# Two more pairs of early products at the head of each SwiGLU, and left factors of the first down group kept whole

## The chip, the cores and the metric

The kernel runs on one core of a Trainium2 chip. The metric is the device time of one execution in microseconds (us). TensorE is called PE below, its weight loads PEld; VectorE is DVE, ScalarE is ACT, GpSimd is POOL, and SP is the engine whose queue issues the DMAs.

## The reference, cut to what matters

One encoder block on x of 1024 tokens by 1024 columns, all in float32: a SwiGLU with an RMS norm before and after it, a mixer of two attentions, and a second SwiGLU of the same form.

```python
def swiglu(x, w_gate, w_up, w_down):          # 1024 -> 2816 -> 1024
    return (jax.nn.silu(x @ w_gate) * (x @ w_up)) @ w_down

f1 = swiglu(rms_norm(h, ffn1_pre_g), ffn1_w_gate, ffn1_w_up, ffn1_w_down)
h = h + 0.5 * rms_norm(f1, ffn1_post_g)
mix = hybrid_mixer(rms_norm(h, mix_pre_g), ...)
h = h + rms_norm(mix, mix_post_g)
f2 = swiglu(rms_norm(h, ffn2_pre_g), ffn2_w_gate, ffn2_w_up, ffn2_w_down)
h = h + 0.5 * rms_norm(f2, ffn2_post_g)
```

## The kernel before

**Splits and seven products.** Every float32 factor is split into a rounded high part and a rest (ACT copies the high part, DVE or POOL subtracts it), and a product takes three matmuls: high by high, high by rest, rest by high. Both SwiGLUs (`ffn`, called once for each) use a scheme of seven products of half blocks in place of eight (the Strassen kind): products 0 to 6 of sums and differences of the quarters.

**Gate and up.** The 2816 hidden columns are 11 pieces `p` of 256. A unit `(p, m)` is the gate (m = 0) or up (m = 1) weight of one piece; `units` lists the 22 of them. Each unit has seven products of 12 matmuls of 512 columns (L675). Products 0 and 1 need only blocks 0 and 1 of the transposed input, made from tokens 0 to 511; the other five need blocks 2 to 6, made from tokens 512 to 1023 and from differences (L414, transposes L426, rests L431). `seq` is the order of the products on PE: at its start products 0 and 1 of the first two units, then unit by unit. `loads` brings the weights of a unit in two halves of 512 KB (`raw_tok` bounds how many), `combos` makes the sums of weight quarters on DVE (L615, L619, L622, L626), `one` makes a split weight `wt` (ACT L648, DVE L649; `w_tok` bounds how many). `step` adds the partial results: a copy of product 0 (`m1`, L744), then L760, L771, L780, L793 and L800 on DVE. `unit_tok` lets two units be open.

**Hidden values.** `hidden` takes the finished quarters of a piece, makes their sums (L849 to L851, L856), splits the seven left factors of the down product (ACT L825, DVE L828) and stores them as high part and rest in the DRAM tensor `hs` (L829, 512 KB each).

**Down.** Five groups `g` of two pieces, seven products each, in the order 0, 5, 1, 4, 6, 2, 3; each has four token tiles `tt` of six matmuls (L1079). `left` loads a factor `ha` (1 MB, L942), `right` splits a weight `wdb` (ACT L521, POOL L522) out of `rawd` (L900) or of sums `td` (DVE L919 to L929). The large buffers that `ha` and `wdb` take are those that the input blocks held, so a first-group factor can be loaded when the last unit has used a block. `evac` adds the products into `acc` and `bacc` (L1026, L1028). After the last product of the last group `fix` adds `bacc` to three quarters: one on DVE (L1037), two at once on POOL (L1039). The eleventh piece is a plain product (L1103 on, its additions L1118), then comes the norm behind the SwiGLU (`postnorm`: L488, L499, L307, L309, L512).

**What sets the order.** The program is written by a planner (`Plan`): processes ask for an engine with a rank (low first) and an assumed duration, and the order in which they are served becomes the instruction order of each engine. Each engine then runs its list in order: an instruction that waits holds up all behind it. In `ffn`, weight splits and combinations have rank 7, the input's chain rank 3, `left` rank 6, `right` rank 7.

Of the kernel before, what the change touches and what calls it, by code (L numbers as in the profile page):

```python
# [19 lines left out]
P = 128  # L20
# [90 lines left out]

AT_BUFFERS = 7712
HELD = 4


class Event:
# [9 lines left out]
class Plan:  # L126
# [17 lines left out]
    def spawn(self, gen, rank=5):  # L144
        self.alive.add(gen)
        self._at(self.now, lambda: self._step(gen, rank))
# [73 lines left out]
def _build(tc, es, a, consts, out, dbg):  # L220
# [16 lines left out]
    def slot(shape, dt=F32, name="u"):  # L237
        return sb.tile(shape, dt, tag="u", bufs=NU, name=nm(name))
# [26 lines left out]
    def act(n, fn):  # L265
        return ("act", 0.04 + n * 0.00088, fn)

    def dve(n, fn):
        return ("dve", 0.15 + n * 0.00105, fn)
# [4 lines left out]
    def pool(n, fn):  # L274
        return ("pool", 0.16 + n * 0.0021, fn)

    def dma(kb, fn):
        return ("dma", kb / 350.0, fn)
# [236 lines left out]
    def raw_tile(w, r0, nk, c0, n):  # L515
        t = slot([P, nk, n], name="raw")
        load(t, w[r0 : r0 + nk * P, c0 : c0 + n].rearrange("(k p) c -> p k c", p=P))
        return t
# [23 lines left out]


    def ffn(X, wg, wu, wd, post, hs, hp, started=None, room=None):
        raw_tok, w_tok, hl_tok = Tokens(4 if room is None else 3), Tokens(6 if room is None else 2), Tokens(3)

        def more():
            yield room
            plan.release(raw_tok, 1)
            plan.release(w_tok, 4)  # L550

        if room is not None:
            spawn(more(), 7)
# [1 line left out]
        units = [(p, m) for p in range(NP) for m in range(2)]  # L555


        seq = [(units[0], 0), (units[1], 0), (units[0], 1), (units[1], 1)]
        for n, u in enumerate(units):
            if n > 1:  # L560
                seq.append((u, 0))
            if n:
                seq += [(units[n - 1], 3), (units[n - 1], 2)]
            if n > 1:
                seq.append((u, 1))
            seq += [(u, 5), (u, 6), (u, 4)]
        seq += [(units[-1], 3), (units[-1], 2)]
        raws = {u: ([None, None], [Event(), Event()]) for u in units}
        ws = {(*u, i): (Box(), Event()) for u in units for i in range(7)}
        unit_tok = Tokens(2)  # L570
        big_tok = Tokens(0)
        sgs = {p: Box() for p in range(NP)}
        for bx_ in sgs.values():
# [9 lines left out]

        def loads():
            yield 0.5
            for p, m in units:
                for kh in range(2):
                    yield raw_tok
                    bx, ev = raws[p, m]

                    def ld():
                        bx[kh] = raw_tile((wg, wu)[m], 512 * kh, 4, 256 * p, 256)

                    yield dma(512, ld)
                    plan.set(ev[kh])
            yield from down_loads()

        def prep():
            sums = {}

            def begin(u):
                rs, ev = raws[u]
                bx = sums[u] = Box()
                bx.L = L = lambda c, k: rs[k][:, :, c * P : (c + 1) * P]
                bx.made = made = [Event() for _ in range(4)]
                bx.read2 = Event()
                bx.used = used = [Event(4), Event(4)]

                def combos():
                    yield ev[0]  # L610
                    yield ev[1]
                    s12 = slot([P, 2, 4, P], name="s12")
                    bx.s1, bx.s2 = s1, s2 = s12[:, 0], s12[:, 1]
                    bx.s3 = s3 = half_slot([P, 4, P], name="s3")
                    yield dve(512, lambda: V.tensor_add(s1, L(1, 0), L(1, 1)))  # L615
                    plan.set(made[0])
                    plan.set(used[0])
                    plan.set(used[1])
                    yield dve(512, lambda: V.tensor_sub(s2, s1, L(0, 0)))  # L619
                    plan.set(made[1])  # L620
                    plan.set(used[0])
                    yield dve(512, lambda: V.tensor_sub(s3, L(0, 0), L(1, 0)))  # L622
                    plan.set(made[2])
                    plan.set(used[0])
                    yield bx.read2
                    yield dve(512, lambda: V.tensor_sub(s2, L(0, 1), s2))  # L626
                    plan.set(made[3])
                    plan.set(used[1])

                def free(kh):  # L630
                    yield used[kh]
                    plan.release(raw_tok)

                bx.combos = combos
                for kh in range(2):
                    spawn(free(kh), 7)

            def one(u, i):
                bx, wx = sums[u], ws[*u, i]
                ev = raws[u][1]  # L640
                yield {0: ev[0], 1: ev[1], 2: bx.made[3], 3: ev[1], 4: bx.made[0], 5: bx.made[1], 6: bx.made[2]}[i]
                L = bx.L
                src = {
                    0: lambda: L(0, 0), 1: lambda: L(0, 1), 2: lambda: bx.s2, 3: lambda: L(1, 1),
                    4: lambda: bx.s1, 5: lambda: bx.s2, 6: lambda: bx.s3,
                }[i]()
                w = wx[0].w = slot([P, 2, 4, P], F32R, "wt")
                yield act(512, lambda: A.copy(w[:, 0], src))  # L648
                yield dve(512, lambda: V.tensor_sub(w[:, 1], src, w[:, 0]))  # L649
                if i == 5:  # L650
                    plan.set(bx.read2)
                if i in (0, 1, 3):
                    plan.set(bx.used[0 if i == 0 else 1])
                plan.set(wx[1])

            for u, i in seq:
                if u not in sums:
                    begin(u)
                if i == 1:
                    spawn(sums[u].combos(), 7)  # L660
                yield w_tok
                spawn(one(u, i), 7)
            yield from down_prep()
# [51 lines left out]
        def step(u, i, ub):  # L715
# [21 lines left out]
            if i == 0:  # L737
# [2 lines left out]

                def m1():
                    def cp():
                        ub.uu = slot([P, 2, 512], name="uu")
                        A.copy(ub.uu[:, 0, :], ub.b1)  # L744

                    yield act(512, cp)
                    plan.set(ub.m1)
# [6 lines left out]
            elif i == 5:  # L754
# [2 lines left out]

                def first():
                    yield ub.m1
                    yield dve(512, lambda: V.tensor_add(u2(), ub.b6, u2()))  # L760
                    plan.release(B1)
                    plan.set(ub.added[0])

# [48 lines left out]
        def hidden(p):  # L812
# [4 lines left out]
            def one(src, evs, dst):  # L817
# [12 lines left out]
                plan.release(hl_tok)  # L830
                plan.set(stored[p])

            if p == NP - 1:
                for n, (c, j) in enumerate(((0, 0), (0, 1), (1, 0), (1, 1))):
                    dst = hp[P * c : P * c + P].rearrange("p (s c) -> p s c", s=2)[:, :, 512 * j : 512 * j + 512]
                    spawn(one(h(n), [hid[p][n]], dst), 5)
                return
# [48 lines left out]
        us = {(g, i): (Box(), Event(2)) for g in range(NGR) for i in range(7)}  # L886
        Y = [None] * NT
        bacc = [None] * 4
        fixed = [Event() for _ in range(NT)]
        plain = [(Box(), Event(2)) for _ in range(2)]  # L890

        def down_loads():
# [13 lines left out]
        def prep_group(g):  # L906
# [29 lines left out]

            def left(i):
                bx, ev = us[g, i]

                def ld():  # L940
                    bx.a = big([P, 2, 2, 512], name="ha")
                    load(bx.a.bitcast(F32).rearrange("p q s c -> p q (s c)"), hs[(i * (NP - 1) + 2 * g) * P : (i * (NP - 1) + 2 * g + 2) * P].rearrange(  # L942
                        "(q p) c -> p q c", p=P))

                yield dma(1024, ld)
                plan.set(ev)
# [76 lines left out]
        def evac(g, i, tt, ps, ev, tok):  # L1023
            o = dst(KIND[i], tt)
            if g == 0 and i in FIRST:
                yield act(512, lambda: A.copy(o, ps))  # L1026
            else:
                yield dve(512, lambda: V.tensor_add(o, o, ps))  # L1028
            plan.set(ev)
            if tok is not None:  # L1030
                plan.release(tok)
            if g == NGR - 1 and i == 3:
                spawn(fix(tt), 2)

        def fix(tt):
            yield pdone[tt]
            yield dve(512, lambda: V.tensor_add(Y[tt][:, 512:], Y[tt][:, 512:], bacc[tt]))  # L1037
            plan.set(fixed[tt])
            yield pool(1024, lambda: G.tensor_add(  # L1039
                Y[tt + 4].rearrange("p (n c) -> p n c", n=2), Y[tt + 4].rearrange("p (n c) -> p n c", n=2),  # L1040
                bacc[tt][:, None, :].broadcast_to([P, 2, 512]),
            ))
            plan.set(fixed[tt + 4])

        pdone = [Event() for _ in range(4)]

        def down():
            for g in range(NGR):
                evs = {}
                banks = {}  # L1050
                for s, i in enumerate(ORDER):
# [4 lines left out]
                    for tt in range(4):  # L1056
# [24 lines left out]

                        yield pe(6 * 512, write)
                        e = evs[i, tt] = Event()
                        if g == NGR - 1 and i == 2:
                            e = evs[i, tt] = pdone[tt]
                        tok = None
                        if i not in MID:
                            tok = B1 if on_b else (S2 if tt % 2 == 1 else None)
# [1525 lines left out]
```

## Time and profile before

| | |
|---|---|
| median of 3 runs | 2476.06 us (2475.08 to 2478.7) |
| the profiled execution | 2472.7 us, span from first to last instruction 2470.5 us |
| PE busy | 2310.1 us, 94% of the span, 11096 matmuls and transposes |
| PEld, DVE, ACT, POOL busy | 1928.9, 1602.3, 1042.7, 798.0 us |
| mean granted PE clock | 0.968 of full speed |
| DMA | 360.64 MB, mean 146 GB/s |

The profile is of one execution. Times in it count from the first instruction. "Busy" of PE includes modelled ends of pipelined matmuls, so a PE that is busy throughout may still run at half clock; the granted clock stands beside it (1.00 is 2.4 GHz). The first SwiGLU lies at about 0 to 707 us, the mixer up to about 1772 us, the second SwiGLU behind it.

### The profile page before, as it was taken

Reading aid. Unit: us, or ns where it says so; the run is one execution under the profiler, and the core shown is the slowest. Engines: PE = TensorE matmul, PEld = TensorE weight load, DVE = VectorE, ACT = ScalarE, POOL = GpSimd, SP = SyncE. Lnnn points to the kernel's source line nnn. Section 1 sums busy time; section 2 is a strip of 40 time slices with the busy share of each in tenths; the row PEclk is TensorE's granted clock in tenths of the full one; section 3 lists DMA queues with packets and bytes.
Section 4 is the critical chain, followed back from the end, with each engine's and each line's share of the span. In section 5 each row is a group of like instructions: output and inputs, shape, how many; then the busy total and the mean of one; then the engine's idle time right before and its main releaser. Section 6 shows DMA issues by size and latency. Waiting matters only on the chain. (4 is left out here: it accounts for less than half of the span.)

```text
span 2470.5 us, 30753 instructions
## 1 busy us (share of the span) xinstructions
PE 2310.1 (94%) x11096; PEld 1928.9 (78%) x11096; DVE 1602.3 (65%) x2667; ACT 1042.7 (42%) x1966; POOL 798.0 (32%) x600
## 2 busy tenths in 40 slices
PE   6999999999979999999998898988889999998996
PEld 4888888778869987888887777766678888877885
DVE  7887877756582105665666767258877877774657
ACT  6343434332153336666664555455343433433211
POOL 2000000354384445665623223566200000023535
PEclk8999999999989999999999999999989999999998
DMA  4243443677342132131232323665333534447762
GB/s 154 103 168 131 170 154 128 244 307 267 135 164 76 60 103 92 38 83 50 66 97 67 85 74 98 206 242 193 131 124 128 183 128 153 162 179 289 286 216 102
DMA packets 188823, 360.64 MB, mean 146 GB/s; under 512 B 32448, under 2 KB 104640, under 8 KB 188160
## 3 DMA queue, kind: packets, MB, share of 16 engines
q1 hardware_dynamic: 188672, 358.69, 42.5%
q8 instruction: 87, 1.43, 0.2%
q14 instruction: 64, 0.52, 0.1%
HBM read 237.92 MB, written 120.72 MB: 145 GB/s over the span
## 5 line engine op out<-in xcount | busy, mean ns | idle before, releaser
L675 PE MATMUL s<-xh,wt 128*128 128x512 f32 x1408 | 452.3, 392 | 13.2 <-DVE uu L771 12.2
L522 POOL TENSOR_TENSOR wdb<-rawd,wdb 128x1024 fp32r<-128x1024 f32 x34 | 87.0, 2562 | 957.9 <-ACT wdb L521 957.9
L675 PE MATMUL b<-xh,wt 128*128 128x512 f32 x1056 | 344.1, 393 | 1.8 <-DVE wt L649 0.8
L675 PEld LDWEIGHTS s<-xh,wt 128*128 128x128 f32 x1408 | 265.9, 189 | 71.9 <-issue 13.3
L675 PE MATMUL s<-xl,wt 128*128 128x512 f32 x704 | 275.4, 391 | 0.0
L675 PEld LDWEIGHTS b<-xh,wt 128*128 128x128 f32 x1056 | 199.8, 189 | 44.4 <-DVE wt L649 1.2
L675 PE MATMUL b<-xl,wt 128*128 128x512 f32 x528 | 207.0, 392 | 0.4 <-DVE xl L431 0.4
L1079 PE MATMUL b<-wdb,ha 128*128 128x512 f32 x864 | 203.2, 390 | 2.2 <-POOL wdb L522 2.2
L1079 PE MATMUL s<-wdb,ha 128*128 128x512 f32 x816 | 196.7, 396 | 8.6 <-POOL wdb L522 4.8
L1079 PEld LDWEIGHTS b<-wdb,ha 128*128 128x128 f32 x864 | 162.3, 188 | 36.8 <-POOL wdb L522 3.1
L1079 PEld LDWEIGHTS s<-wdb,ha 128*128 128x128 f32 x816 | 156.0, 192 | 43.9 <-POOL wdb L522 5.7
L1442 PE MATMUL b<-xh,wh 128*128 128x512 f32 x384 | 162.7, 424 | 1.4 <-DVE o L1963 0.8
L1913 POOL TENSOR_TENSOR p<-p,rd 128x1024 f32<-128x1024 f32 x64 | 122.4, 1921 | 118.0 <-DVE rd L1910 112.7
L649 DVE TENSOR_TENSOR wt<-s,wt 128x512 fp32r<-128x512 f32 x176 | 120.4, 712 | 53.7 <-ACT wt L648 53.7
L675 PEld LDWEIGHTS s<-xl,wt 128*128 128x128 f32 x704 | 133.2, 189 | 27.0
L1442 PE MATMUL b<-xl,wh 128*128 128x512 f32 x384 | 153.3, 399 | 0.0
L1442 PE MATMUL b<-xh,wl 128*128 128x512 f32 x384 | 153.2, 399 | 0.0
L522 POOL TENSOR_TENSOR wdb<-td,wdb 128x1024 fp32r<-128x1024 f32 x40 | 105.9, 2653 | 73.9 <-ACT wdb L521 73.9
L426 PE MATMUL b<-cst,p 128*128 128x128 f32 x768 | 107.2, 280 | 22.0 <-DVE ptd L431 14.8
L522 POOL TENSOR_TENSOR wl<-raw,wh 128x512 fp32r<-128x512 f32 (+3 forms) x88 | 109.7, 1263 | 53.8 <-ACT wh L521 46.3
L426 PEld LDWEIGHTS b<-cst,p 128*128 128x128 f32 x768 | 90.1, 143 | 39.8 <-DVE ptd L431 17.4
L648 ACT CAST wt<-s 128x512 fp32r<-128x512 f32 x176 | 103.2, 621 | 34.1 <-DVE s L619 16.8
(295 smaller groups left out, 5015.6 us busy)
## 6 DMA issues: line engine op xcount, KB each, us to landing
hs_d<-hl SPq DMA_DIRECT2D x140, 512.0 KB
ha<-hs_d SPq DMA_DIRECT2D x70, 1024.0 KB
raw<-in_ffn_w_gate_dram SPq DMA_DIRECT2D x44, 512.0 KB
raw<-in_ffn_w_up_dram SPq DMA_DIRECT2D x44, 512.0 KB
rawd<-in_ffn_w_down_dram SPq DMA_DIRECT2D x44, 512.0 KB
raw<-in_w_in_dram SPq DMA_DIRECT2D x28, 512.0 KB
h<-res SPq DMA_DIRECT2D x16, 512.0 KB
lg_d<-lg SPq DMA_DIRECT2D x32, 256.0 KB
```

Of the source, the lines that this page charges most:

```text
L426: T.transpose(b[:rows, i * P : (i + 1) * P], src(i), ident)
L522: yield pool(n, lambda: G.tensor_sub(lo, src, hi))
L648: yield act(512, lambda: A.copy(w[:, 0], src))
L649: yield dve(512, lambda: V.tensor_sub(w[:, 1], src, w[:, 0]))
L675: T.matmul(out(), l, r, start=(first and k == 0 and n == 0), stop=(k == 3 and n == 2), skip_group_check=True,)
L1079: T.matmul(ps, l, r, start=(fresh and n == 0), stop=(n == 5), skip_group_check=True)
L1442: T.matmul(bs.ps, l, r, start=(part == 0 and n == 0), stop=(part == 7 and n == 2))
L1913: yield pool(S, lambda: G.tensor_tensor(bx.p, bx.p, bx.rd.broadcast_to([P, S]), op=ALU.mult))
```

## The change

Four units (`EARLY`) instead of two have their products 0 and 1 at the head of `seq`. Their weights come by loads of their own, `ers`: 128 columns by all 1024 rows, 512 KB, one for each early unit; `head_of` splits them. The full weights of these units are loaded as well, afterwards. `combos` of an early unit starts at its product 5 instead of its product 1. In the second SwiGLU, `w_tok` starts with 4 instead of 2. The copy `m1` goes into a half-sized buffer. `unit_tok` lets four units be open. For the first two pieces `hidden` stores the factors unsplit (`whole`, 256 KB, no ACT or DVE work); `left` of the first down group loads them (512 KB) and splits them (ACT, then DVE, 1024 columns each). `fix` runs on DVE alone, one quarter at a time, each as soon as its last product is added and `bacc` is complete (`bdone`, at product 5 of the last group).

```diff
+EARLY = 4
+W0 = 4
-        raw_tok, w_tok, hl_tok = Tokens(4 if room is None else 3), Tokens(6 if room is None else 2), Tokens(3)
+        raw_tok, w_tok, hl_tok = Tokens(4 if room is None else 3), Tokens(6 if room is None else W0), Tokens(3)
...
-            plan.release(w_tok, 4)
+            plan.release(w_tok, 6 - W0)
...
-        seq = [(units[0], 0), (units[1], 0), (units[0], 1), (units[1], 1)]
+        early = units[:EARLY]
+        seq = [(early[n + j], i) for n in range(0, EARLY, 2) for i in range(2) for j in range(2)]
...
-        unit_tok = Tokens(2)
+        unit_tok = Tokens(EARLY)
+        ers = {u: (Box(), Event()) for u in early}
...
+            for p, m in early:
+                yield raw_tok
+                ex, ee = ers[p, m]
+
+                def ld():
+                    ex.r = raw_tile((wg, wu)[m], 0, NK, 256 * p, P)
+
+                yield dma(512, ld)
+                plan.set(ee)
...
+            def head_of(u, i):
+                (ex, ee), wx = ers[u], ws[*u, i]
+                yield ee
+                w = wx[0].w = slot([P, 2, 4, P], F32R, "wt")
+                src = ex.r[:, 4 * i : 4 * i + 4, :]
+                yield act(512, lambda: A.copy(w[:, 0], src))
+                yield dve(512, lambda: V.tensor_sub(w[:, 1], src, w[:, 0]))
+                plan.set(wx[1])
+                if i == 1:
+                    plan.release(raw_tok)
...
-                        ub.uu = slot([P, 2, 512], name="uu")
-                        A.copy(ub.uu[:, 0, :], ub.b1)
+                        ub.c1 = half_slot([P, 512], name="m1")
+                        A.copy(ub.c1, ub.b1)
...
+            def whole(src, evs, dst):
+                for e in evs:
+                    yield e
+                yield dma(256, lambda: load(dst[:, 0, :], src))
+                plan.set(stored[p])
+
+            if p < 2:
+                one = whole
...
+                if g == 0:
+
+                    def ld0():
+                        bx.a = big([P, 2, 2, 512], name="ha")
+                        bx.f = bx.a.bitcast(F32)[:, :, 1, :]
+                        load(bx.f, hs[i * (NP - 1) * P : (i * (NP - 1) + 2) * P, 0:512].rearrange("(q p) c -> p q c", p=P))
+
+                    yield dma(512, ld0)
+                    yield act(1024, lambda: A.copy(bx.a[:, :, 0, :], bx.f))
+                    yield dve(1024, lambda: V.tensor_sub(bx.a[:, :, 1, :], bx.f, bx.a[:, :, 0, :]))
+                    plan.set(ev)
+                    return
...
-        def fix(tt):
-            yield pdone[tt]
-            yield dve(512, lambda: V.tensor_add(Y[tt][:, 512:], Y[tt][:, 512:], bacc[tt]))
-            plan.set(fixed[tt])
-            yield pool(1024, lambda: G.tensor_add(
...
+            if g == NGR - 1 and i == 5:
+                plan.set(bdone[tt])
+            if g == NGR - 1 and i in (6, 2, 3):
+                spawn(fix(i, tt), 2)
...
+        def fix(i, tt):
+            yield bdone[tt]
+            o = dst(KIND[i], tt)
+            yield dve(512, lambda: V.tensor_add(o, o, bacc[tt]))
+            plan.set(fixed[tt + (0 if i == 2 else 4)])
```

## Rows read from the trace of the kernel before

**Rows 1.** The page's first line: span and instructions.
```profile
span 2470.5 us, 30753 instructions
```
**Rows 2.** Busy time in stretches: length, busy of each engine, clock, DMA share, GB/s.
```profile
0.00:42.00 42.00, 21.13 (x78) 14.55 (x78) 31.52 (x53) 24.86 (x47) 15.57 (x28) 0.89 0.54 176
42.00:60.50 18.50, 16.73 (x85) 13.28 (x85) 16.18 (x28) 11.83 (x22) 0.00 (x0) 0.87 0.31 94
60.50:447.00 386.50, 386.50 (x1706) 319.45 (x1704) 305.09 (x521) 148.45 (x270) 0.00 (x0) 1.00 0.41 147
447.00:463.00 16.00, 16.00 (x72) 13.22 (x71) 14.69 (x13) 9.96 (x15) 8.56 (x4) 1.00 0.69 246
463.00:482.00 19.00, 12.90 (x50) 10.03 (x49) 11.95 (x11) 3.93 (x6) 11.64 (x4) 0.82 0.51 183
482.00:515.00 33.00, 32.88 (x146) 26.88 (x144) 7.29 (x12) 11.67 (x22) 0.00 (x0) 1.00 1.00 385
1772.50:1807.50 35.00, 18.32 (x77) 13.73 (x77) 32.29 (x49) 18.08 (x33) 9.00 (x14) 0.62 0.48 165
```
**Rows 3.** PE's waits over the execution: total us, times, longest.
```profile
PE s L675 <- DVE uu L771: 12.2, 2, 6.1
PE b L283 <- DVE acc L1118: 10.9, 6, 3.1
...
PE s L1079 <- POOL wdb L522: 4.8, 2, 2.5
...
PE s L1079 <- DVE bacc L1028: 3.3, 2, 2.2
```
**Rows 4.** Busy time in stretches again, of L675's matmuls alone: PE, PEld, clock, DMA.
```profile
0.00:27.60 27.60, 5.85 (x12) 3.80 (x12) 1.00 0.82 267
42.00:60.50 18.50, 10.74 (x37) 6.97 (x37) 0.87 0.31 94
...
1726.00:1762.00 36.00, 12.15 (x48) 8.85 (x48) 1.00 0.44 155
```
**Rows 5.** Timeline of DVE in the first head: start, duration, instruction.
```profile
20.84 0.68 DVE L615 TENSOR_TENSOR s<-raw,raw 128x512 f32<-128x512 f32 x1
...
43.14 0.69 DVE L649 TENSOR_TENSOR wt<-raw,wt 128x512 fp32r<-128x512 f32 x1
```
**Rows 6.** Timeline of PE in the first head: eight transposes at full clock.
```profile
53.64 1.03 PE L426 MATMUL b<-cst,xt 128*128 128x128 f32 x8
```
**Rows 7.** Timeline of PE between the mixer and the second SwiGLU.
```profile
1761.52 11.04 PE L283 MATMUL b<-wo,mt 128*128 128x512 f32 x48
...
1795.01 1.09 PE L426 MATMUL b<-cst,xn 128*128 128x128 f32 x4 [6.23 <-DVE xn L451]
```
**Rows 8.** DVE's groups by shape, 60 to 440 us: busy, mean ns.
```profile
L828 DVE TENSOR_TENSOR hl<-hs,hl 128x512 fp32r<-128x512 f32 x36 | 24.0, 687 | 0.0
```
**Rows 9.** Timeline of SP, the DMA queue, in the first down group.
```profile
485.75 8.34 SPq L942 DMA_DIRECT2D ha<-hs_d  x7
```
**Rows 10.** Timeline of POOL: in the first down product and behind the last.
```profile
466.23 2.33 POOL L522 TENSOR_TENSOR wdb<-rawd,wdb 128x1024 fp32r<-128x1024 f32 x1
...
515.17 5.53 POOL L522 TENSOR_TENSOR wdb<-rawd,wdb 128x1024 fp32r<-128x1024 f32 x2 [36.71 <-ACT wdb L521]
...
2422.89 10.30 POOL L1039 TENSOR_TENSOR acc<-acc,bacc 128x1024 f32<-128x1024 f32 x4 [20.76 <-DVE acc L1028]
2433.15 1.28 POOL L488 TENSOR_TENSOR xn<-acc,p 128x512 f32<-128x512 f32 x1
```
**Rows 11.** Timeline of DVE where the first SwiGLU turns to its down product.
```profile
455.44 1.21 DVE L919 TENSOR_TENSOR td<-rawd,rawd 128x1024 f32<-128x1024 f32 x1
...
466.30 3.35 DVE L929 TENSOR_TENSOR td<-rawd,td 128x1024 f32<-128x1024 f32 x1 [1.64 <-POOL wdb L522]
469.57 0.68 DVE L771 TENSOR_TENSOR uu<-s,uu 128x512 f32<-128x512 f32 x1
```
**Rows 12.** Timeline of DVE in the norm behind the second SwiGLU.
```profile
2435.37 2.27 DVE L512 SCALAR_TENSOR_TENSOR res<-xn,rstd,res 128x1024 f32<-128x1024 f32 x1 [3.84 <-POOL rstd L309]
```

More of the change, by code (lines that the diff above doesn't have):

```diff
@@ L555, in ffn @@
         units = [(p, m) for p in range(NP) for m in range(2)]
-        seq = [(units[0], 0), (units[1], 0), (units[0], 1), (units[1], 1)]
+        early = units[:EARLY]
+        seq = [(early[n + j], i) for n in range(0, EARLY, 2) for i in range(2) for j in range(2)]
         for n, u in enumerate(units):
-            if n > 1:
+            if n >= EARLY:
                 seq.append((u, 0))
@@ L563, in ffn @@
                 seq += [(units[n - 1], 3), (units[n - 1], 2)]
-            if n > 1:
+            if n >= EARLY:
                 seq.append((u, 1))
@@ L606, in begin @@
                 bx.read2 = Event()
-                bx.used = used = [Event(4), Event(4)]
+                n = 3 if u in early else 4
+                bx.used = used = [Event(n), Event(n)]
                 def combos():
@@ L656, in prep @@
             for u, i in seq:
+                if u in early and i < 2:
+                    yield w_tok
+                    spawn(head_of(u, i), 7)
+                    continue
                 if u not in sums:
                     begin(u)
-                if i == 1:
+                if i == (5 if u in early else 1):
                     spawn(sums[u].combos(), 7)
@@ L759, in first, with add @@
                     yield ub.m1
-                    yield dve(512, lambda: V.tensor_add(u2(), ub.b6, u2()))
+                    def add():
+                        ub.uu = slot([P, 2, 512], name="uu")
+                        V.tensor_add(u2(), ub.b6, ub.c1)
+                    yield dve(512, add)
                     plan.release(B1)
@@ L888, in ffn @@
         bacc = [None] * 4
-        fixed = [Event() for _ in range(NT)]
+        fixed = [Event(1 if t < 4 else 2) for t in range(NT)]
         plain = [(Box(), Event(2)) for _ in range(2)]
@@ L1031, in evac @@
                 plan.release(tok)
-            if g == NGR - 1 and i == 3:
-                spawn(fix(tt), 2)
-        def fix(tt):
-            yield pdone[tt]
-            yield dve(512, lambda: V.tensor_add(Y[tt][:, 512:], Y[tt][:, 512:], bacc[tt]))
-            plan.set(fixed[tt])
-            yield pool(1024, lambda: G.tensor_add(
[L1040 to L1045, printed above, removed]
+            if g == NGR - 1 and i == 5:
+                plan.set(bdone[tt])
+            if g == NGR - 1 and i in (6, 2, 3):
+                spawn(fix(i, tt), 2)
+        bdone = [Event() for _ in range(4)]
+        def fix(i, tt):
[3 more added lines that the diff above has]
+            plan.set(fixed[tt + (0 if i == 2 else 4)])
         def down():
@@ L1083, in down @@
                         e = evs[i, tt] = Event()
-                        if g == NGR - 1 and i == 2:
-                            e = evs[i, tt] = pdone[tt]
                         tok = None
```

## The prediction

> **What bounds the kernel now.** I read first the page's first line: the profiled execution has a span of 2470.5 us [rows 1] in a time of 2472.7 us, so 2.2 us lie around the span. All sums below are made against this execution. The median of the runs shown, 2476.06 us, is 3.4 us above it, and I add these 3.4 us at the end.
>
> Then busy time by stretches, cut where the stages change [rows 2]. The reader is to see that from 60.5 to 447 us, gate and up of the first SwiGLU, PE is busy for all of 386.5 us at a clock of 1.00: there PE is the bound, a matmul costs 386.5 / 1706 = 0.227 us, and a product of 12 costs 2.72 us. At that pace nothing that other engines do less of is worth anything, and work that PE does earlier, while it would wait, is worth its whole 2.72 us a product. PE waits in four kinds of place. From 0 to 42 us it is busy 21.13 us, and from 42 to 60.5 us 16.73 of 18.5 us at a clock of 0.87, beside a DVE with 16.18 us. Before the second SwiGLU, from 1772.5 to 1807.5 us, it is busy 18.32 of 35 us at a clock of 0.62, with DVE at 32.29 us. Where gate and up turn to down, from 463 to 482 us, it is busy 12.90 of 19 us.
>
> The waits of PE give the names [rows 3]: two waits of 6.1 us for L771, one in each SwiGLU; 4.8 and 3.3 us in the down products for L522 and L1028; and 10.9 us behind the last down products for L1118.
>
> **The change part by part: the heads.** Of the early products only the first of the first SwiGLU runs before 27.6 us (12 matmuls), and 37 matmuls more run from 42 to 60.5 us; in the second SwiGLU all four, 48 matmuls, run before 1762 us, while the mixer still ends [rows 4]. What holds them in the first head is DVE: between the combination at 20.84 us and the split at 43.14 us DVE runs nothing but the input's chain, which has the better rank [rows 5]. The change postpones such combinations, so that their places can go to early splits. I take it that one more product comes before 42 us, into time in which PE waits: 2.7 us. From 42 to 60.5 us PE's real work is 37 x 0.227 = 8.4 us and 48 transposes (85 less 37) of some 0.11 us, as the eight that take 1.03 us with a modelled end of 0.27 us show [rows 6], 5.3 us: 13.7 of 18.5 us. So 4.8 us are slack that products in store can fill; I take 4.0. First head: -6.7 us. Bounds: +2 us, if a product whose split is late stands ahead of transposes in PE's list; -10.9 us, four products of 2.72 us.
>
> In the second head PE is full up to the mixer's last matmuls, 48 from 1761.52 us, and then waits in ten pieces, one of them 6.23 us [rows 7]. A product placed before 1772.5 us delays the mixer's end by as much as it saves later. The four new ones have to fall into the 35 - 18.32 = 16.7 us that are idle. At half clock a product takes 2 x 2.72 = 5.4 us, so three fit, and each saves its 2.72 us later: -8.2 us. They are queued among the transposes that feed a DVE which is 92% busy, and the sums that product 5 needs now start later on that same DVE; I take 2.2 us for both: -6 us. Bounds: +3 us and -10.9 us.
>
> **Work moved out of gate and up.** In each SwiGLU 14 rest splits of 0.69 us [rows 8] leave DVE, as many copies leave ACT, and 14 stores halve. They lie beside the full PE of 60.5 to 447 us, where DVE has 81 us free: worth nothing. If that cover were gone they would be worth 14 x 0.69 = 9.6 us. The four extra loads of 2 MB lie there too, at a DMA share of 0.41, and cost nothing. In the first 20 us as many loads of 512 KB are issued as before, in other shapes. The new home of the copy and the four open units change only what may wait, in a stretch in which nothing does: 0.
>
> **The first down group.** Two effects oppose each other. From 482 to 515 us the DMA engines are full, share 1.00 at 385 GB/s. SP issues seven loads of factors of 1 MB in 8.3 us [rows 9] before the weights of the second group; POOL stands idle for 36.71 us until 515.17 us for want of these weights [rows 10], and behind it come the 4.8 and 3.3 us of PE. Of the first group's seven loads about three belong to this crowd, and each loses 512 KB: 1.57 MB at 385 GB/s are 4.1 us by which the weights land earlier. I take -4 us for each SwiGLU, bounded by 0 and by all of the waits.
>
> Against it stand seven new copies on ACT, which is free for more than half of 447 to 482 us, and seven new subtractions of 1024 columns on DVE. The last three fall into 482 to 515 us, where DVE has 25 us free. The first four fall before, where PE already waits 6.1 us for L771. It is late because DVE's list stood at L929, which waited for POOL and then took 3.35 us beside it, where the like L919 took 1.21 us alone [rows 11]. So an early subtraction costs 1.21 us if it meets no POOL work and 3.35 us if it does. Between 447 and 482 us DVE is busy 26.6 of 35 us, and most of the rest lies where PE or POOL is awaited. Four of them cost the path between 0 and 13.4 us; I take one at 3 us, ahead of L771 in DVE's list, with the others in the gaps. Each subtraction also waits for its load and its copy, and behind it on DVE stand the additions that free PE's banks; from 482 us the loads are late. I price that at 0, since PE needs a factor only a product of 5.44 us or more later; the bound is another 3.3 us. SP's list keeps its order. Both SwiGLUs: 2 x (-4 + 3) = -2 us.
>
> Here a rule of the Trainium skill speaks against the change. SBUF — State Buffer, section Who interferes with whom, says that a DVE instruction with two SBUF inputs and a GpSimd instruction that reads SBUF exclude each other: the one that comes second is blocked for the whole of the first. L929's 3.35 us against 1.21 agree. By the rule a subtraction that comes up during a split of POOL costs 1.21 us and up to the whole 2.33 us of that split, and if nothing hides the early four, the sum would be some -8 us instead of what follows; from rows alone that is worked out as a rival.
>
> **Behind the last group.** L1039 holds POOL for 10.30 us; only then comes L488 and then the rstd for which DVE stands idle 3.84 us [rows 10, 12]. Eight more additions on DVE replace it. Each of the last three products leaves DVE four additions in 5.44 us (24 matmuls), so the new ones fit at no cost; without that cover they would be 8 x 0.6 = 4.8 us. Behind the second SwiGLU nothing follows but this chain: -3.8 us. Behind the first the mixer's own start follows, and I take PE's longest stop there, -3 us. Bounds: 0 and -3.8 us each.
>
> **Sum.** -6.7 - 6 - 2 - 3.8 - 3 = -21.5 us: 2472.7 - 21.5 = 2451.2 us, and with the 3.4 us 2454.6, say 2455 us. A difference under 0.2%, 5 us, is about what a measurement of this kernel cannot tell from no change.
>
> **The rivals.** *All of it comes.* Both heads give four products, 21.8 us, the loads 8 us, the tails 7.6 us, and DVE's gaps hide the subtractions: -37.4 us, 2439 us. For it speak the idle PE of both heads; against it the DVE that is nearly full in each.
>
> *The heads give little.* DVE, not PE's order, sets the end of a head, so the new splits come when PE is busy again: -2 us in the first, 0 in the second, where the new products go ahead of the mixer's end. With -2 and -6.8 us for the rest: -10.8 us, 2465 us. For it speaks that DVE is 90% busy in both heads.
>
> *The early subtractions meet POOL.* POOL is busy 20.2 of the 35 us from 447 to 482 us [rows 2], a share of 0.58, so the mean of one is 1.21 + 0.58 x 2.14 = 2.45 us; four, with nothing to hide them, are 9.8 us in each SwiGLU in place of my 3. With the rest as forecast: -21.5 + 2 x 6.8 = -8 us, 2468 us. DVE's few free us there speak for it. It is what the Trainium skill's rule of exclusion (SBUF — State Buffer, Who interferes with whom) would bring about.
>
> *No change.* The little heads, and the early subtractions cost 8 us in each down group: -2 + 0 - 8 + 16 - 6.8 = about -1 us, 2475 us.
>
> *Slower.* One mechanism: in DVE's list the four early subtractions stand ahead of L771, each beside a split of POOL, at 3.35 us. That is 13.4 us in each SwiGLU. With the little heads, the 8 us of the loads and the tails: 26.8 - 2 - 8 - 6.8 = +10 us, 2486 us. It decides from 8.4 us for each SwiGLU. Against it speaks that L771 has a better rank than `left`.
>
> **How the numbers follow.** Forecast 0.44, with a range of its own of 2447 to 2462 us; all of it 0.15; little heads 0.17; subtractions that meet POOL 0.07; no change 0.08; slower 0.09. The range from 2436 to 2472 us holds the first four, 0.83. Faster by over 0.2%: 0.83; within: 0.08; slower: 0.09.
>
> **What would show it.** Right: 96 matmuls of early products in each head; PE full from before 55 us; POOL's L522 of the second group starting well before the end of the first; no L1039; no stop of 3.8 us before the first L512. Wrong: early products still behind 43 us or before the mixer's end; L771 later than 6 us after its product; new waits of PE for `ha` split on DVE; an input chain that ends later than 62 and 1812 us by more than the products save.

## The result and the profile after

The changed kernel takes 2433.76 us (median of 4 runs, 2431.0 to 2435.61) against 2476.28 us: a ratio of 0.9829 with an interval of 0.9815 to 0.9843, 42.5 us less. A second set of runs, beside other kernels, gave 2434.32 us and 0.983. That is faster, as forecast, but 2.2 us below the range and nearly double the forecast 21 us.

The page's first line of the changed kernel; the one of before is in [rows 1]:

```profile
span 2430.7 us, 30689 instructions
```

The waits of PE (total us, times, longest), to be read beside [rows 3]:

```profile
PE s L706 <- DVE uu L807: 9.0, 2, 4.6
PE b L285 <- DVE acc L1171: 4.9, 3, 3.7
```

L706 and L807 are L675 and L771 of before, L1171 is L1118. What is no longer there is the news: in the down products PE has no wait for POOL's weights and none for `bacc`. Busy time by stretches, first for two stretches of the changed kernel that answer to 463 to 482 and 482 to 515 us in [rows 2], then for two of the kernel before that were not shown:

```profile
462.00:480.00 18.00, 13.61 (x50) 10.51 (x50) 16.64 (x11) 7.53 (x9) 10.71 (x4) 0.81 0.41 135
480.00:513.00 33.00, 33.00 (x148) 27.31 (x147) 24.28 (x21) 19.05 (x29) 18.11 (x7) 1.00 0.92 350
```
```profile
515.00:520.00 5.00, 2.32 (x6) 1.60 (x7) 1.15 (x1) 3.52 (x5) 4.83 (x2) 0.77 1.04 413
520.00:525.00 5.00, 5.00 (x14) 3.86 (x13) 1.49 (x3) 0.00 (x0) 5.00 (x3) 0.55 0.76 295
```

Before, PE does 6 matmuls in one 5 us and 14 in the next, where 22 fit. From 520 to 525 us it counts as busy for all 5.00 us, but at a granted clock of 0.55. So a wait of 2.5 us is followed by matmuls at about half clock, and the list of waits shows only about half of the loss. After, POOL has splits to do from 483 us on, where it stood idle for 36.71 us before [rows 10], and PE is full at clock 1.00.

To place all of the time, I cut each kernel's profiled execution at the same pieces of PE's work, by the starts of its matmuls: the 384th and 1752nd gate/up product matmul, the 24th, 384th and 840th down product matmul, the first L1442 and the last L283 of the mixer, and the same in the second SwiGLU. So "first head" runs from the start to the 384th gate/up matmul, a "turn" from the 1752nd gate/up matmul to the 24th of the down product, "down group 1" from there to the 384th, and "behind it" from the 840th to the mixer; the last column ends with DVE's last instruction. Lengths in us; gate/up (310.1 to 310.3) and the later down groups (103.36) are left out, being the same in every kernel to 0.2 us. "again" is the second profile of the changed kernel.

```
          first  turn   down   be-    mixer   second turn   down   be-
          head   to     group  hind           head   to     group  hind
                 down   1      it                    down   1      it
before   136.41  35.19  90.08 166.67  930.20  112.45 36.32  90.79  41.66
fix      137.05  35.38  92.97 163.06  931.38  112.49 36.27  90.42  35.99
order    137.83  35.79  81.60 166.69  929.72  113.57 35.71  81.60  41.67
cost     136.77  35.04  81.60 166.66  933.01  113.63 35.36  81.60  41.69
down     137.52  38.67  81.60 166.70  926.64  113.79 38.61  81.60  41.67
noheads  136.75  38.31  81.60 162.65  923.93  113.81 38.34  81.60  35.99
heads    134.39  37.33  95.73 166.68  925.60  108.31 37.37  95.93  41.67
swap     134.95  37.56  81.60 162.97  927.48  108.19 37.41  81.60  35.98
after    135.62  34.13  81.60 163.13  924.82  108.73 34.73  81.60  35.99
again    135.93  34.39  81.60 163.33  922.58  108.08 34.45  81.60  35.99
late     135.31  32.95  81.60 163.55  927.02  107.91 32.86  81.60  35.98
own      133.59  31.83  81.60 162.35  925.57  108.54 31.44  81.60  35.98
```

From before to after the columns give -0.8, -1.1, -8.5, -3.5, -5.4, -3.7, -1.6, -9.2 and -5.7 us, and gate/up -0.3: the 39.8 us by which the spans differ (the profiled execution of before lies below its median, so the medians differ by more). The largest entries are the two first down groups, 17.7 us, for which my whole forecast was 2 us. 81.60 us there is 360 matmuls at 0.227 us: nothing is lost any more.

### The profile page after: what moved, and what is told of

Read it like the earlier page. It is cut to its first block, busy times and chain, and to the rows that moved or that the text cites. A ratio compares the mean times of both kernels' runs of the same rounds, so it can differ in the third digit from the quotient of the medians.

```text
span 2430.7 us, 30689 instructions
## 1 busy us (share of the span) xinstructions
PE 2294.6 (94%) x11096; PEld 1920.7 (79%) x11096; DVE 1609.8 (66%) x2669; ACT 1044.0 (43%) x1952; POOL 784.1 (32%) x592
## 5 line engine op out<-in xcount | busy, mean ns | idle before, releaser
L706 PE MATMUL s<-xh,wt 128*128 128x512 f32 x1408 | 453.8, 393 | 10.2 <-DVE uu L807 9.0
L706 PE MATMUL b<-xh,wt 128*128 128x512 f32 x1056 | 345.7, 394 | 0.7 <-ACT xh L432 0.6
L706 PEld LDWEIGHTS s<-xh,wt 128*128 128x128 f32 x1408 | 266.2, 189 | 69.8 <-DVE uu L807 10.7
L706 PE MATMUL s<-xl,wt 128*128 128x512 f32 x704 | 275.7, 392 | 0.0
L706 PEld LDWEIGHTS b<-xh,wt 128*128 128x128 f32 x1056 | 200.9, 190 | 44.0 <-ACT xh L432 1.0
L706 PE MATMUL b<-xl,wt 128*128 128x512 f32 x528 | 207.7, 393 | 0.9 <-DVE xl L433 0.9
L1134 PE MATMUL s<-wdb,ha 128*128 128x512 f32 x816 | 190.5, 389 | 0.0
L706 PEld LDWEIGHTS s<-xl,wt 128*128 128x128 f32 x704 | 133.3, 189 | 27.4
L675 ACT CAST wt<-s 128x512 fp32r<-128x512 f32 x176 | 104.2, 617 | 113.9 <-DVE s L635 59.0
```

Source lines behind the costliest of these rows:

```text
L706: T.matmul(out(), l, r, start=(first and k == 0 and n == 0), stop=(k == 3 and n == 2), skip_group_check=True,)
L1134: T.matmul(ps, l, r, start=(fresh and n == 0), stop=(n == 5), skip_group_check=True)
```

## The experiments

**heads, down, fix: each part alone.** The edits are the change's own: `heads` has EARLY, W0, `head_of` and the home of `c1`; `down` has `whole` and `ld0`; `fix` has `bdone` and the final additions on DVE.

> The heads alone: two products of four units, with the kernel before's split stores, loads and final additions. Theory A, read from the shifts between the two traces: 0.9 us come from the first head and 4.8 us from the second, and 3.4 us more appear in the mixer between 761 and 1726 us for a reason that is not known; -6 us if those 3.4 us belong to another part, -9 us if to the heads. Theory B, the recorded sum: -12.7 us.

> The first down group alone: factors whole in DRAM, loaded at half size and split by ACT and DVE; heads and final additions as before. Theory A: the weights of the second down group come in time, PE no longer stops there and no longer runs at half clock behind the stop; from its 24th to its 384th matmul the first group takes 81.6 us in place of 90.1 and 90.8 us, and L771's wait is 1.1 and 1.6 us shorter: -20 us. Theory B, the recorded sum: -8 us of loads and +6 us of early subtractions, -2 us.

> The final additions alone: eight more on DVE, none on POOL. Theory A, from the shifts: 4.5 us behind the first SwiGLU and 5.7 us behind the second, -10 us. Theory B, the recorded sum: -3.0 - 3.8 = -6.8 us.

Measured against 2478.41 us: `heads` 2474.06 us (ratio 0.9989, 0.9977 to 1.0), `down` 2460.25 us (0.9928, 0.9913 to 0.9943), `fix` 2466.94 us (0.9948, 0.9931 to 0.9964). `down` and `fix` (18.2 and 11.5 us by the medians) are near theory A. `heads` (4.4 us by the medians, 2.7 by the ratio) is a miss for both: its heads are shorter by 2.0 and 4.1 us, but its first down groups are longer by 5.6 and 5.1 us and its turns by 2.1 and 1.0 us. The waits of PE in `heads`:

```profile
PE s L706 <- DVE uu L807: 14.9, 2, 7.7
PE s L1115 <- POOL wdb L524: 11.6, 4, 4.0
...
PE s L1115 <- ACT wdb L523: 7.3, 4, 2.0
```

They are the old waits, longer: what the heads give, a down group without the other part takes back. Why the first down groups lose more behind the heads was not looked into. The waits of `down` show the price of the early subtractions, and DVE's timeline in its first turn the reason:

```profile
PE s L675 <- DVE uu L771: 17.5, 2, 8.7
```
```profile
466.66 2.83 DVE L828 TENSOR_TENSOR hl<-sg,hl 128x512 fp32r<-128x512 f32 x1
469.41 4.49 DVE L957 TENSOR_TENSOR ha<-ha 128x1024 fp32r<-128x1024 f32 x2
473.83 0.68 DVE L771 TENSOR_TENSOR uu<-s,uu 128x512 f32<-128x512 f32 x1
474.43 1.21 DVE L937 TENSOR_TENSOR td<-rawd,td 128x1024 f32<-128x1024 f32 x1
```

Two subtractions, 4.49 us together, stand right ahead of L771, and the turns are 3.5 and 2.3 us longer. The fourth combination (L929 before, L937 here) has gone behind L771. My 3 us for one early subtraction in each SwiGLU was about the sum of these, partly by luck.

**order: the same bytes in another order.** One rank in the kernel before.

```
-                spawn(left(i), 6)
+                spawn(left(i), 8 if g else 6)
```

> The kernel before with one rank changed: in SP's queue the loads of factors of the second and later down groups stand behind the loads of down weights (rank 8 in place of 6). No byte, no split and no addition changes. Theory A1 (the gain of the down group is one of order in SP's queue, not of bytes): the stops for L522 and L1028 vanish and the first groups lose little of the 8.5 and 9.2 us: -10 to -17 us. Theory A2 (it is one of bytes: the smaller loads free the DMA engines): the same bytes land by the same time, PE now waits for factors in place of weights: within 4 us of no change.

2456.81 us, ratio 0.9911 (0.9896 to 0.9925): 21.6 us, theory A1, and 4.6 us beyond its top. Both first down groups take 81.60 us, as after the change, with stores and loads of before. A2 falls. SP's timeline of `order`, where seven loads of factors stood in a row before [rows 9]:

```profile
487.77 2.35 SPq L942 DMA_DIRECT2D ha<-hs_d  x2
490.21 1.36 SPq L900 DMA_DIRECT2D rawd<-in_ffn_w_down_dram  x2
491.67 0.59 SPq L942 DMA_DIRECT2D ha<-hs_d  x1
492.35 0.42 SPq L900 DMA_DIRECT2D rawd<-in_ffn_w_down_dram  x1
```

**cost: one number of the planner.** The kernel before, with the first group's loads booked at half their size and still moving all of it.

```
-                yield dma(1024, ld)
+                yield dma(1024 if g else 512, ld)
```

> The kernel before with one number of the planner changed: it books a load of factors of the first group at 512 KB, while 1 MB is still moved; no instruction is added or removed. The program's order alone changes: SP's weights of the second group no longer stand behind eight loads of factors. Theory A1 (order): most of the 17.6 us that the first down groups lose between their 24th and 384th matmul comes back, -10 to -20 us. Theory A2 (bytes): nothing is moved less, so within 5 us of no change.

2451.98 us against 2476.94 us, ratio 0.9904 (0.9888 to 0.992): 25 us, theory A1 and 5 us beyond its top, more than half of the change's gain, from a number that no engine sees. The table places 17.7 us of it in the first down groups; its profiled execution is the slowest of the four (2457.51 us), with a mixer of 933.01 us, so where the other 7 us lie is not shown. Its busy time in the stretch of [rows 2] that has a DMA share of 1.00 and in the one behind it:

```profile
482.00:515.00 33.00, 33.00 (x148) 27.33 (x147) 19.05 (x16) 16.57 (x26) 11.77 (x6) 1.00 0.97 353
515.00:535.00 20.00, 20.00 (x90) 16.58 (x89) 13.98 (x19) 4.78 (x6) 15.62 (x6) 1.00 0.84 289
```

**bytes: the change with the bytes of before.** Each load of factors of the first group moves its 512 KB twice.

```
-                        load(bx.f, hs[...])
+                        load(bx.a.bitcast(F32)[:, :, 0, :], src)
+                        load(bx.f, src)
```

> The changed kernel, but each load of factors of the first group moves its 512 KB twice, into both halves of its buffer, so that the bytes are those of before in the order of the change; the planner books it as before, and SP issues 14 more. Theory A1 (order): the weights still come ahead of the crowd, 2431 to 2438 us against 2434 us. Theory A2 (bytes): the stops of PE for L524 come back, 6 to 8 us in each SwiGLU, 2446 us or more.

2434.16 us, ratio 0.983 (0.9815 to 0.9844): no different from the changed kernel. Busy time where the change has a DMA share of 0.92:

```profile
480.00:513.00 33.00, 33.00 (x148) 27.34 (x147) 16.97 (x20) 18.05 (x29) 10.79 (x5) 1.00 1.01 370
```

The DMA engines are full again, PE does not notice, and both first down groups take 81.60 us. Of the gain of the down groups nothing is due to fewer bytes loaded.

**swap: heads and final additions with `order` in place of the change's down part.**

```
 (before, with the edits of heads and fix, and)
-                spawn(left(i), 6)
+                spawn(left(i), 8 if g else 6)
```

> The heads and the final additions of the change, with the kernel before's split stores and loads of 1 MB, and the rank that puts the loads of factors behind the loads of weights in SP's queue. Theory A1 (order): the down groups need nothing of the change's new stores and splits: within 6 us of the changed kernel, 2428 to 2440 us. Theory A2 (bytes): 2446 us or more, by the bytes that are not saved.

2439.84 us, ratio 0.9856 (0.9839 to 0.9873): 6.1 us above the changed kernel, at the edge of A1. The table says where: the two turns are 3.4 and 2.7 us longer, in the mixer, which scatters, it loses 2.7 us, and elsewhere it differs by less than 1 us. DVE's timeline of `swap` in the first turn:

```profile
461.19 1.22 DVE L960 TENSOR_TENSOR td<-rawd,rawd 128x1024 f32<-128x1024 f32 x1
466.97 3.35 DVE L965 TENSOR_TENSOR td<-rawd,td 128x1024 f32<-128x1024 f32 x1 [4.56 <-POOL wdb L524]
470.25 0.68 DVE L807 TENSOR_TENSOR uu<-s,uu 128x512 f32<-128x512 f32 x1
```

As before the change [rows 11], the fourth combination waits for POOL ahead of the addition that PE needs. In the changed kernel the fourth combination (L973) stands behind L807.

**late: one split moved out of L807's way.** The changed kernel with L864's split behind L807. Two waits in the planner do it.

```
                     plan.set(ub.added[1])
+                    if u == units[-1]:
+                        plan.set(last_second)
...
+                if g == 0:
+                    yield last_second
+                    yield 1.5
                 yield dve(1024, lambda: V.tensor_sub(tb.t3, R(1, 1), R(0, 1)))
```

> The changed kernel with one instruction moved in DVE's list: the split of 2.83 us for the last rows, L864, stands behind L807 in place of ahead of it. Theory A (what is left of PE's wait where gate and up turn to down, 4.4 and 4.6 us, is DVE's list): L807 comes 2.8 us earlier in each SwiGLU, 2427 to 2430 us. Rival (POOL's splits beside it stretch whatever stands ahead of L807, or PE's next products lack banks anyway): within 2 us of 2434 us.

2433.24 us, ratio 0.9825 (0.9811 to 0.984): by time the rival. The turns are 1.2 and 1.9 us shorter than in the changed kernel. That is too little to be measured, and less than the 2.8 us moved, because PE now waits for the next addition as well (L707, L808 and L819 are L706, L807 and L816 of the changed kernel); its waits:

```profile
PE s L707 <- DVE uu L808: 4.3, 2, 2.2
PE s L707 <- DVE uu L819: 2.7, 2, 1.5
```

**noheads: the change without its heads.** The edits of `down` and `fix` together.

> The change without the heads: first down group and final additions as changed, two early units as before. Theory A (the heads are worth 2 us in the first and 6.5 us in the second SwiGLU, and beside that they happen to shorten L807's wait from 8.7 to 4.4 us where the down part is in): 2434 + 8.5 + 8.6 = 2451 us. Rival, the parts add up as they were measured alone: 2477 - 17.8 - 12.9 = 2446 us.

2449.36 us, ratio 0.9891 (0.9876 to 0.9905), between the two and nearer to theory A; the interval, 3.6 us to either side, holds both, so the time alone doesn't decide. Beside the rest of the change the heads are worth 15 us (2449.36 - 2434.32); alone they were worth 2.7 (0.11%; 4.4 by the medians), with an interval that reaches to none. By the table only 1.1 and 5.1 us of the 15 lie in the heads themselves; 4.2 and 3.6 us lie in the turns.

**own and again: L965 no longer waits for POOL.** `own` is `swap` with one more buffer; `again` is the changed kernel.

```
+                tb.t4 = tb.t2 if g else slot([P, 2, 512], name="td")
-                yield dve(1024, lambda: V.tensor_sub(tb.t2, R(1, 0), tb.t2))
+                yield dve(1024, lambda: V.tensor_sub(tb.t4, R(1, 0), tb.t2))
```

The wait on `read5` ahead of it falls away in the first group, and the split of factor 3 reads `tb.t4`.

> The kernel of the order, heads and final additions (2439.8 us), with one more buffer: the fourth combination of the first group's weights, L965, writes a tile of its own in place of the one that POOL's split still reads, and so no longer waits for POOL. Theory A (L807's wait of 7.4 and 7.6 us is DVE's list, which stands at L965 for 4.56 us): L807 comes some 4.4 us earlier in each SwiGLU, 2429 to 2433 us. Rival (POOL's splits stretch the same subtractions in any order, as with L864 moved): 2436 to 2440 us.

> The changed kernel once more, on the chip of the two beside it: 2431 to 2436 us by every theory.

`own` takes 2429.05 us (ratio 0.9814, 0.9798 to 0.983), `again` 2434.32 us, on the same chip: theory A. Against `swap` the turns are 5.7 and 6.0 us shorter. The time is 5.3 us below the changed kernel's, though their intervals overlap. DVE's timeline of `own`, and its wait:

```profile
458.65 1.22 DVE L960 TENSOR_TENSOR td<-rawd,rawd 128x1024 f32<-128x1024 f32 x1
459.78 3.42 DVE L967 TENSOR_TENSOR td<-rawd,td 128x1024 f32<-128x1024 f32 x1
463.12 0.68 DVE L807 TENSOR_TENSOR uu<-s,uu 128x512 f32<-128x512 f32 x1
```
```profile
PE s L706 <- DVE uu L807: 4.8, 2, 2.6
```

The subtraction still takes 3.42 us beside POOL, but the 4.56 us of waiting ahead of it are gone, and the turns are 31.83 and 31.44 us long. This version has none of the change's new splits of factors.

## Why the prediction was wrong, point by point

**The down groups: the step that failed.** It reads "SP's list keeps its order", and with it the -4 us for 1.57 MB at 385 GB/s, less 3 us for the subtractions; the first down groups came out 8.5 and 9.2 us shorter. I had seen the crowd of seven loads ahead of the weights and counted how much shorter it would be. Even that count was off: SP had issued six loads of factors before the crowd, and the kernel asks for them group by group, so one of the seven belongs to the first group and not three. The step that failed is the order. The planner books a load by its size, and with half the size booked it writes another order: weights go out between the loads of factors. SP's timeline of the changed kernel:

```profile
490.73 0.55 SPq L999 DMA_DIRECT2D ha<-hs_d  x1
491.34 1.33 SPq L944 DMA_DIRECT2D rawd<-in_ffn_w_down_dram  x2
492.76 0.45 SPq L999 DMA_DIRECT2D ha<-hs_d  x1
493.26 0.50 SPq L944 DMA_DIRECT2D rawd<-in_ffn_w_down_dram  x1
```

`cost` and `order` show that the order is enough, `bytes` that the smaller loads add nothing to it. The second error is in the bound, "all of the waits": I took the waits of PE as the loss. In the first SwiGLU they are 4.5 us between the 24th and 384th matmul (0.26, 2.54, 1.14 and 0.52), and the stage lost 8.5 us (90.08 - 81.60); of the rest 2.8 us fell right behind the wait of 2.54 us, where the rows of 515 to 525 us show the lowered clock and most matmuls start 0.43 us apart in place of 0.227.

**The early subtractions.** About right in sum where they stand alone (`down`). In the changed kernel no cost shows: its turns are 1.1 and 1.6 us shorter than before. I had not foreseen two things in DVE's list. The fourth combination, for which DVE stood still before, comes behind the addition that PE needs in every kernel with the new splits (L937 in `down`, L973 in the changed kernel) and ahead of it in every kernel without them (`heads` and `swap` too), so the splits move it and not the heads. And in the changed kernel only two subtractions come before L807, 15 and 8 us ahead of it, and none right ahead of it as in `down`. Why the planner's order came out so was not looked into; nothing in the prediction led to it. DVE's timeline of the changed kernel:

```profile
459.06 1.23 DVE L993 TENSOR_TENSOR ha<-ha 128x1024 fp32r<-128x1024 f32 x1
...
467.45 0.68 DVE L807 TENSOR_TENSOR uu<-s,uu 128x512 f32<-128x512 f32 x1
468.05 2.78 DVE L993 TENSOR_TENSOR ha<-ha 128x1024 fp32r<-128x1024 f32 x1
470.76 1.21 DVE L973 TENSOR_TENSOR td<-rawd,td 128x1024 f32<-128x1024 f32 x1
...
473.90 1.22 DVE L993 TENSOR_TENSOR ha<-ha 128x1024 fp32r<-128x1024 f32 x1
```

L993 takes 2.78 us where it comes up during a split of POOL (466.94 to 469.75 us), and 1.22 us where it starts ahead of one (473.90 against 474.42 us), which agrees with the rule of the Trainium skill that the prediction cites (SBUF — State Buffer, Who interferes with whom).

**The first head: too large.** Forecast -6.7 us, measured -0.8; the mean of the seven profiles with the heads (135.1, the table's and `bytes`) against that of the six without (137.1) is -1.9. The rival of little heads had -2. Its products in the changed kernel, PE and PEld by stretch:

```profile
0.00:42.00 42.00, 8.64 (x24) 5.71 (x24) 0.93 0.71 210
42.00:56.00 14.00, 7.89 (x24) 5.47 (x24) 0.86 0.31 102
56.00:69.00 13.00, 11.52 (x50) 9.34 (x51) 1.00 0.30 85
```

Before 42 us 24 product matmuls are done, against 14 in the kernel before: nearly the one product that I had. But by 56 us it is 48, four products, in both kernels. The other four run when PE is nearly full anyway; the slack of 4.8 us was not filled.

**The second head: right in sum, wrong in place.** Forecast -6 us, measured -3.7, and -5.1 between the means of the same profiles (108.2 against 113.3). I had three products at half clock among the transposes behind the mixer (PE's waits there are nine, not ten). All four run one after another right behind the mixer's last matmuls, which end at 1753.15 us, and at full clock; no product matmul runs from 1770.5 to 1791 us:

```profile
1742.50:1770.50 28.00, 11.51 (x48) 8.86 (x48) 0.99 0.27 95
```

That moves four products, 10.9 us, out of the later work. But the last transpose of the input starts 45.5 us behind the mixer's last matmul in place of 38.9 us, which takes 6.6 us back. My 2.2 us for that was too small.

**Behind the last groups: too small behind the second.** Forecast -3 and -3.8 us, measured -3.5 and -5.7; the second is the same to 0.01 us in every kernel with this edit. I priced the one visible stop of DVE. The better price was in the row of POOL [rows 10]: its first L488 came 7.8 us after the 840th down matmul (2433.15 - 2425.34), and now L490 comes 2.6 us after it (2393.90 - 2391.28), 5.2 us sooner:

```profile
2393.90 1.61 POOL L490 TENSOR_TENSOR xn<-acc,p 128x512 f32<-128x512 f32 x1 [25.82 <-DVE acc L1171]
```

**The mixer: not in the sum, and not settled.** It is 5.4 us shorter in the changed kernel, but it scatters: 922.6 to 927.5 us in kernels with the heads, 923.9 to 933.0 without. `order`, which edits nothing there, runs the part from the start of the last L2251 to the first product of the second SwiGLU 2.9 us faster than before (1719.36 - 1545.86 against 1726.25 - 1549.83). The heads, whose first products stand at its end, are not needed for it: `noheads`, the rest of the change without them, has 923.9 us, as short as the changed kernel's 924.8 and 922.6. What shortens it stays open.

Put together: heads -4.5 where -12.7 were forecast, turns and first down groups -20.3 where -2 were, ends -9.2 where -6.8 were, and the mixer's -5.4. That the total lies near the rival in which all of it comes (2439 us) is chance: its terms are not these.

## What to carry to other kernels

When a planner writes the order of a queue from booked sizes, an edit that changes a booking changes the order for everything behind it; compare the queue's list before pricing the bytes, and try the booking alone first. A wait of TensorE costs more than its length where the clock falls behind it, so price a stage by its matmuls against the full-clock pace, not by the sum of its waits. And parts that share an in-order engine do not add up: here the heads were worth 3 to 4 us alone and 15 beside the rest.

## What was not expected of the hardware

A DMA share of 1.01 in the first down group did not slow PE at all (`bytes`, 33.00 of 33 us at clock 1.00), while about as many bytes in another order, with the crowd of loads ahead of the weights, cost 8.5 to 14.3 us (90.08 to 95.93 us against 81.60). In the kernels without that order all first down groups take 81.60 us to the hundredth.
